# Modulation with w_mod blocks as stationary operands, first projections chunk by chunk, one SSD product per head for both directions

## The chip, the cores and the metric

The kernel runs on one core of a Trainium2 chip. TensorE is called PE here, VectorE DVE, ScalarE ACT, GpSimd POOL, and SP issues the transfers. The metric is the device time of one execution in microseconds; the time given for a kernel is the median of several runs.

## The reference

A two-layer generator backbone over 1024 latent tokens and 256 context tokens of width 1024. Per layer:

```python
mod_l = jax.nn.silu(c) @ w_mod[l] + b_mod[l]          # and mod_c from c_ctx: 3 x 1024 columns
h_l = rmsnorm(x, norm_w[l]) * (1.0 + sc_l) + sh_l     # h_c likewise for the context
(fu, fg, q, k, v, ag, z, xbc, dt, gt) = jnp.split(h @ w_in[l], split_at, axis=-1)
# Fourier mixing of fu, differential attention of q, k, v, SSD of xbc and dt,
# each times silu of its gate path; merged by sigmoid(gt), projected, added to x
```

The SSD runs in both directions over chunks of 128 positions (2 groups of 4 heads, head width 64). Its part inside a chunk is

```python
cb = jnp.einsum('bclgn,bcsgn->bcgls', cc, bc)
y_diag = jnp.einsum('bcgls,bgrcls,bcsgrp->bclgrp', cb, lmat, x * dt)   # lmat = exp of decay, triangular
y = y_f + rev(y_b) + d_skip[:, None] * xs
```

The context goes first through the SSD; in layer 1 (the last) only its final states are used, not its outputs.

## The kernel before

All activations live in 28 slots of 128 x 1288 fp32 (tiles `ar`). Projections are computed with both operands split into an f16 high and an f16 low part: each pair of 128x128 weight tile and activation block gives three f16 matmuls (`acc3`), and `projT` for a chunk of 512 tokens is 8 blocks of these, 24 matmuls. Weights arrive as fp32 in `raw`, and are squared, scaled and split into `w` by ACT and DVE (`fetch`). The 1280 tokens are ten tiles in three chunks: 512, 512 and the context's 256.

Instructions are not issued in the order of the code. Five generators (m: the main branches; p: projections; f: merges and the layer's end; e: gates; g: modulation of layer 1) hand operations to a list scheduler in Python, which keeps a model clock per engine, gives each operation a priority (its number minus `BIAS` of its thread; weights are `w`), lets a generator run until `AHEAD` operations of it are pending, and places PSUM banks. DVE and ACT may wait for a nearly ready operation of higher priority (`HOLD`). What it writes out is fixed: each engine then runs its list in order on the chip. So a changed cost or table moves instructions everywhere.

At the start (`mod0`), for each of eight blocks k of the contraction, two 128x1024 pieces of w_mod arrive: `part` 1 (scale) and 0 (shift). For part 1 and k < 7 DVE accumulates piece times the per-partition value of silu(c) for both conditions in `acc`; the rest goes to PE with the 128x2 block of silu(c) as the stationary operand and 512 columns of w_mod moving, and gives rows of 2 x 1024. `partition_sums` (products with a column of ones) and 16 transposes bring both into columns; `mod_finish` makes `ab`, the scale and bias by which ACT turns transposed, normalized x into h (`norm_T`), and DVE splits h into high (a cast) and low (a subtraction). Chunk 0 is handled in thread p (tiles `scrp`), the other two in f (`scrf`). `proj_fu` projects the Fourier inputs, one half of a weight tile at a time over all chunks.

In `ssd_scan` each chunk loads the decay rows of both directions and four heads (`rv`, 128 x 2 x 4 x 128), ACT makes relu and exp of them, DVE multiplies by the upper and lower triangle of C and B's product (`cb`), and PE multiplies each of the eight 128x128 blocks (stationary) with x times dt (`xd`, in `scrm`), forward and backward accumulating in one place of `y`.

Of the kernel before, what the change touches and what calls it, by code (L numbers as in the profile page):

```python
# [14 lines left out]
AF = mybir.ActivationFunctionType  # L15
ALU = mybir.AluOpType
# [20 lines left out]
U_SC = 2.0 ** -16  # L37
# [6 lines left out]
NSLOT = 28  # L44
NW = 8
RAW = 2
BIAS = {'m': 1200, 'p': 400, 'w': 600, 'f': 0, 'e': -50000, 'g': -100000}
AHEAD = {'m': 100, 'p': 150, 'f': 40, 'e': 54, 'g': 6}
MAXB = {'m': 4, 'p': 3, 'f': 3, 'e': 1, 'w': 1, 'g': 1}
LEAST = (1, 1)  # L50
WLIM = {'p': 2, 'f': 4, 'e': 1}
# [366 lines left out]
class Builder:  # L418
# [281 lines left out]
    def mod_finish(self, L, modT):  # L700

        V, l = self.nc.vector, L.l
        pv = self.pv[l]
        V.tensor_tensor(modT, modT, pv[:, 0:16].unsqueeze(2).to_broadcast([128, 16, 2]), ALU.add)
        ab = self.cst.tile([128, 2, 8, 2], F32, name=f"ab{l}")
        V.scalar_tensor_tensor(ab[:, 0], modT[:, 8:16, :], 1.0,
                               pv[:, 24:32].unsqueeze(2).to_broadcast([128, 8, 2]), ALU.add, ALU.mult)
        V.tensor_copy(ab[:, 1], modT[:, 0:8, :])
        f = ab.rearrange("p a k s -> p (a k s)")
        sq = self.small(32)  # L710
        V.tensor_tensor(sq, f, f, ALU.mult)
# [12 lines left out]
        V.tensor_scalar(f, f, S, None, ALU.mult)
        L.ab = ab
# [8 lines left out]
    def mod0(self, L):  # L734

        nc, V = self.nc, self.nc.vector
        row, acc = [self.alloc(), self.alloc()], [self.alloc(), self.alloc()]
        p = [[self.mm(True), self.mm(True)] for _ in range(2)]
        nc.bias['w'] = 0
        for k in range(8):  # L740
            for part in (1, 0):
                yield ('slots', 1)
                s = self.alloc()
                nc.sync.dma_start(s.v(1024), self.A['wm'][0, part, k])
                for i in range(2):
                    if part and k < K_DVE:
                        a, c = acc[i].v(1024), self.cs[:, k, i:i + 1]
                        if k == 0:
                            V.tensor_scalar(a, s.v(1024), c, None, ALU.mult)
                        else:  # L750
                            V.scalar_tensor_tensor(a, s.v(1024), c, a, ALU.mult, ALU.add)
                    else:
                        self.mul(p[part][i][:2], self.cs[:, k], s.v(1024)[:, i * 512:i * 512 + 512], k == K_DVE * part, k == 7)
                s.drop()
            if k == 1:
                self.consts()
            if k == 3:
# [6 lines left out]
            if k == K_DVE:
                t = self.mm(True)
                self.partition_sums(acc, t[:, 32:48])
        for part in range(2):
            for i in range(2):
                nc.scalar.activation(row[part].v(1024)[:2, i * 512:i * 512 + 512], p[part][i][:2], AF.Copy)
            for b in range(8):  # L770
                nc.tensor.transpose(t[:, 16 * part + 2 * b:16 * part + 2 * b + 2], row[part].v(1024)[:2, b * 128:b * 128 + 128], self.ident[:2, :2])
        modT = self.cst.tile([128, 16, 2], F32, name="modT0")
        V.tensor_copy(modT.rearrange("p b s -> p (b s)"), t[:, :32])
        V.tensor_tensor(modT[:, 8:].rearrange("p b s -> p (b s)"), modT[:, 8:].rearrange("p b s -> p (b s)"), t[:, 32:48], ALU.add)
        for r in row + acc:
            r.drop()
# [69 lines left out]
    def norm_T(self, L, tiles, xt):  # L846
# [5 lines left out]
        for d in range(8):  # L852
            p = self.tp()
            for i in range(n):
                self.tr(p[:, i * 128:i * 128 + 128], xt[i].v(1024)[:, d * 128:d * 128 + 128])
            t = self.scr() if n > 2 else self.scr2()
            nc.scalar.activation(t[:, :n * 128], p[:, :n * 128], AF.Identity,
                                 scale=L.ab[:, 0, d, st:st + 1], bias=L.ab[:, 1, d, st:st + 1])
            h = L.hT[d][:, :, t0:t0 + n * 128]
            nc.vector.tensor_copy(h[:, 0], t[:, :n * 128])  # L860
            nc.vector.tensor_tensor(h[:, 1], t[:, :n * 128], h[:, 0], ALU.subtract)
            yield
        for s in xt:
# [342 lines left out]
    def toff(t):  # L1206
        return t * 128 if t < 8 else 1028 + (t - 8) * 128

    def conv_block(self, L, w, half, d, blk, res):

        nc, V = self.nc, self.nc.vector
        cp = self.pv[L.l][:, 33 + 6 * blk:39 + 6 * blk]
        yield ('slots', 1)
        xin = self.alloc()
        xv = xin.v(1288)
        for a, b in ((0, 2), (1026, 1030), (1286, 1288)):
            nc.gpsimd.memset(xv[:, a:b], 0.0)
        for c0, cn in CH_ALL:
            p = self.projT(w, L.hT, half, c0, cn)
            o = c0 + 2 if c0 < 1024 else 1030  # L1220
            nc.scalar.activation(xv[:, o:o + cn], p[:, :cn], AF.Copy, scale=d)
            yield
        yield ('slots', 1)
        acc = self.alloc()
        av = acc.v(1284)
        nc.scalar.activation(av, xv[:, 0:1284], AF.Identity, scale=cp[:, 0:1], bias=cp[:, 5:6])
        for k in range(1, 5):
            V.scalar_tensor_tensor(av, xv[:, k:k + 1284], cp[:, k:k + 1], av, ALU.mult, ALU.add)
        nc.scalar.activation(xv[:, 0:1284], av, AF.Tanh)
        V.scalar_tensor_tensor(av, xv[:, 0:1284], 1.0, av, ALU.add, ALU.mult)  # L1230
        xin.drop()
        res.append(acc)

    def ssd_in(self, L, g):
# [25 lines left out]
        r = []  # L1260
# [5 lines left out]
        for t0 in range(0, NT, 4):  # L1266
# [3 lines left out]
                o = self.toff(t0 + i)  # L1270
                self.tr(p[:, i * 128:i * 128 + 128], G.BT.v(1284)[:, o:o + 128])
            nc.scalar.activation(G.bn[:, t0:t0 + tn].rearrange("p t n -> p (t n)"), p[:, :tn * 128], AF.Copy)
        yield from self.conv_block(L, w, 1, d, 6 + g, r)
        G.CT = r[1]
        self.done(L, f'bc{g}')
        yield ('need', (L.l, 'w', f'z{g}'))
# [11 lines left out]
    def ssd_scan(self, L, g):  # L1288
# [30 lines left out]
        for c in [8, 9, 0, 1, 2, 3, 4, 5, 6, 7]:  # L1319
            if c < L.nt:  # L1320
# [7 lines left out]
                for dr in range(2):  # L1328
                    for h in range(4):
                        nc.scalar.activation(rv[:, dr, h], rv[:, dr, h], AF.Relu, scale=-1.0, bias=av[:, dr, h:h + 1])  # L1330
                nc.scalar.activation(row.v(1024), row.v(1024), AF.Exp, scale=-1.0)
                p = self.alt()
                self.mul(p[:, :128], G.BT.v(1284)[:, o:o + 128], G.CT.v(1284)[:, o:o + 128], True, True)
                cb = self.scr()
                V.tensor_tensor(cb[:, 0:128], p[:, :128], self.U, ALU.mult)
                V.tensor_tensor(cb[:, 128:256], p[:, :128], self.L, ALU.mult)
                for dr in range(2):
                    V.tensor_tensor(rv[:, dr], rv[:, dr], cb[:, dr * 128:dr * 128 + 128].unsqueeze(1).to_broadcast([128, 4, 128]),
                                    ALU.mult)
                xd = self.scr()  # L1340
                xdv = xd.rearrange("p (d h q) -> p d h q", d=2, h=4)
                for dr in range(2):
                    V.tensor_tensor(xdv[:, dr], G.x[c].rearrange(h4, q=64), bc4(L.dt, c, dr), ALU.mult)
                yield 5.0
                y, y2 = self.alt(), self.alt()
                for h in range(4):
                    for dr in range(2):
                        self.mul(y[:, h * 64:h * 64 + 64], rv[:, dr, h], xdv[:, dr, h], dr == 0, dr == 1)
                row.drop()
                if H is not None:  # L1350
                    self.mul(y2[:, 256:512], G.CT.v(1284)[:, o:o + 128], H, True, True)
# [75 lines left out]
    def proj_fu(self, L, pair):  # L1427
# [4 lines left out]
        nc.vector.tensor_tensor(cy[:, 0:1], inv, L.inv_h, ALU.mult)  # L1432
        nc.vector.tensor_scalar(cy[:, 1:2], cy[:, 0:1], 2.0 ** 13 * 2.0 ** -7.5, None, ALU.mult)
        nc.vector.tensor_scalar(cy[:, 0:1], cy[:, 0:1], 2.0 ** 13 * 2.0 ** -8.5, None, ALU.mult)
        for j in range(2):
            yield ('slots', 1)
            u = self.alloc()
            for c0, cn in L.chunks:
                yield ('need', (L.l, f'h{c0 // 512}'))
                p = self.projT(w, L.hT, j, c0, cn)  # L1440
                nc.scalar.activation(u.v(1280)[:, c0:c0 + cn], p[:, :cn], AF.Copy, scale=U_SC)
                yield
            L.u[2 * pair + j] = (u, cy)
# [657 lines left out]
```

## Time and profile before

| | |
|---|---|
| median of 3 runs | 2614.3 us (2610.61 to 2615.71) |
| the profiled execution | 2615.48 us, span 2613.7 us |
| mean granted clock of PE | 0.980 of 2.4 GHz |
| busy: PE, DVE, ACT, POOL | 2501.8, 1828.2, 1252.1, 33.7 us |

The span is the time from the first instruction to the last in the profiled execution. Busy time counts an engine once where instructions overlap. A group's busy time is its share of that; its mean is the duration of one instruction by itself, which for pipelined matmuls is longer than what each adds. An fp32 matmul is counted as two instructions. All helpers record at line 400, so groups are told apart by tiles.

### The profile page before, as it was taken

What the parts mean: (1) busy time and instruction counts of PE and PEld (TensorE: products, weight loads), DVE (VectorE), ACT (ScalarE), POOL (GpSimd) and SP (SyncE); (2) the same over time, 40 slices, a digit from 0 to 9 for tenths busy, and PEclk for the clock granted to TensorE, in tenths of its full rate; (3) what the DMA queues carried; (4) which work ended last, traced back from release to release, by engine and by line L of the source; (5) the groups of instructions that cost most, each with busy time, mean ns of one, the idle gap of its engine ahead of it and who ended that gap; (6) DMA issues with size and microseconds to landing.
All of it is one profiled execution on the core that took longest, in us unless ns stands there. A gap on an engine that the chain in (4) does not pass through costs nothing. (4 is left out here: it accounts for less than half of the span.)

```text
span 2613.7 us, 42499 instructions
## 1 busy us (share of the span) xinstructions
PE 2501.8 (96%) x16962; PEld 1565.2 (60%) x16962; DVE 1828.2 (70%) x3783; ACT 1252.1 (48%) x2260; POOL 33.7 (1%) x78
## 2 busy tenths in 40 slices
PE   5999999999999999999999999999999899999998
PEld 2556655666665476576588546545655457556567
DVE  6785665677888468468866687776676748558766
ACT  4543545536654455445423464464544645446321
POOL 0000000000000000000000000000000000000000
PEclk8999999999999999999999999999999899999999
DMA  6331333344356223213632123434342412222451
GB/s 247 112 101 53 86 82 94 90 143 110 84 129 179 68 77 115 68 53 102 230 137 97 43 83 74 111 93 99 98 91 62 123 57 73 93 88 94 155 180 65
DMA packets 256978, 270.61 MB, mean 104 GB/s; under 512 B 181062, under 2 KB 191110, under 8 KB 256780
## 3 DMA queue, kind: packets, MB, share of 16 engines
q1 hardware_dynamic: 256780, 267.89, 34.6%
q8 instruction: 133, 2.18, 0.3%
q14 instruction: 65, 0.53, 0.1%
HBM read 178.02 MB, written 36.88 MB: 82 GB/s over the span
## 5 line engine op out<-in xcount | busy, mean ns | idle before, releaser
L400 PE MATMUL ps<-ar,w 128*128 128x512 f16 (+1 forms) x7200 | 1463.1, 356 | 9.4 <-ACT w L400 6.1
L400 PEld LDWEIGHTS <-w 128*128 128x128 f16 x7200 | 699.5, 98 | 643.0 <-issue 20.3
L400 PEld LDWEIGHTS <-ar 128*128 128x128 f16 x8144 | 668.1, 98 | 256.7 <-issue 36.7
L400 PE MATMUL ps<-ar,ar 128*128 128x128 f16 (+4 forms) x4420 | 555.9, 277 | 24.7 <-ACT ar L400 14.1
L400 PE MATMUL ps<-w,ar 128*128 128x256 f16 x3312 | 400.8, 273 | 0.4 <-ACT ar L400 0.4
L400 ACT ACTIVATE ar<-ps,s1m,qksc 128x1280 f32<-128x1280 f32 (+1 forms) x144 | 190.1, 1320 | 196.9 <-DVE s1m L400 134.1
L400 DVE TENSOR_REDUCE s1m<-ps 128x1 f32<-128x1280 f32 (+1 forms) x144 | 197.0, 1368 | 92.5 <-PE ps L400 91.8
L400 ACT ACTIVATE w<-raw 128x1024 f16<-128x1024 f32 x145 | 152.4, 1051 | 128.1 <-PE ps L400 75.3
L400 ACT ACTIVATE ar<-ar 128x1280 f16<-128x1280 f32 (+4 forms) x140 | 153.8, 1100 | 102.0 <-DVE ar L400 91.8
L400 DVE SCALAR_TENSOR_TENSOR ar<-ar,pv,ar 128x1284 f32<-128x1284 f32 x64 | 99.4, 1554 | 64.9 <-ACT ar L400 63.5
L400 DVE TENSOR_TENSOR ar<-ar,ar 128x1280 f16<-128x1280 f32 (+3 forms) x116 | 123.4, 1065 | 13.9 <-ACT ar L400 13.5
L400 PE MATMUL ps<-scrm,ar 128*128 128x64 f32 (+1 forms) x720 | 122.3, 305 | 7.1 <-issue 3.3
L400 ACT ACTIVATE ar<-ps 128x128 f32<-128x128 f32 (+6 forms) x196 | 69.7, 387 | 115.4 <-PE ps L400 114.3
L400 ACT ACTIVATE ar<-ps,ds 128x512 f32<-128x512 f32 (+1 forms) x88 | 54.7, 624 | 140.8 <-PE ps L400 136.0
L400 PEld LDWEIGHTS ps<-scrm,ar 128*128 128x128 f32 x720 | 99.1, 198 | 35.2 <-DVE scrm L400 18.4
L400 PE MATMUL ps<-k,ar 128*128 128x128 f32 (+2 forms) x540 | 88.6, 292 | 27.6 <-DVE ar L400 25.9
L400 DVE SCALAR_TENSOR_TENSOR ar<-ar,ps 128x512 f32<-128x512 f32 (+1 forms) x116 | 64.3, 562 | 65.1 <-ACT ar L400 47.8
L400 PEld LDWEIGHTS ps<-k,ar 128*128 128x128 f32 (+1 forms) x540 | 68.8, 163 | 61.6 <-DVE ar L400 31.0
L400 DVE SCALAR_TENSOR_TENSOR ar<-ar,s1m,ar 128x1280 f32<-128x1280 f32 (+1 forms) x72 | 103.1, 1432 | 0.0
L400 ACT ACTIVATE ar<-ar,ar 128x128 f32<-128x128 f32 x288 | 88.1, 388 | 24.3 <-DMA ar<-rows 21.0
L400 DVE SCALAR_TENSOR_TENSOR w<-raw,s1p,w 128x1024 f16<-128x1024 f32 x71 | 89.1, 1279 | 11.3 <-ACT w L400 11.2
L400 ACT ACTIVATE scrf<-ps,ds 128x512 f32<-128x512 f32 (+1 forms) x80 | 51.2, 639 | 86.2 <-PE ps L400 65.2
(215 smaller groups left out, 2049.3 us busy)
## 6 DMA issues: line engine op xcount, KB each, us to landing
raw<-in_wt SPq DMA_DIRECT2D x160, 512.0 KB, 4.6
ar<-in_wm SPq DMA_DIRECT2D x48, 512.0 KB, 5.4
ar<-rows SPq DMA_DIRECT2D x36, 512.0 KB, 3.8
yp<-scrf SPq DMA_DIRECT2D x64, 256.0 KB, 2.3
ar<-in_x SPq DMA_DIRECT2D x20, 512.0 KB, 9.4
gs<-scre SPq DMA_DIRECT2D x32, 256.0 KB, 2.8
scrf<-yp SPq DMA_DIRECT2D x32, 256.0 KB, 2.7
ar<-ar SPq DMA_DIRECT2D x32, 160.0 KB, 2.8
```

The source lines that it names most:

```text
L400: o.fn(*(place(a) for a in o.args), **{k: place(a) for k, a in o.kw.items()})
```

## The change

1. `mod0`: every 128x128 block of both parts is the stationary operand of a product with the 128x2 block of silu(c); all accumulate in 32 columns of one PSUM tile, which a product with a zero operand clears first. The DVE sums, the partition sums, the transposes and the row copies go; the bias is added in the copy out.
2. `norm_T`: the cast of h is done by POOL for groups of four tiles (chunks 0 and 1).
3. `proj_fu`: chunk by chunk, both halves of the weight tile in each chunk.
4. `conv_block`: for C, in layer 1, without the context chunk.
5. `ssd_scan`: forward and backward relu are summed (each is zero where the other counts), so one exp and one decay block serve both directions; `cb` is multiplied with dt of each head and direction beforehand, and each head needs one product, with x itself moving.
6. The scheduler's numbers: `BIAS`, `AHEAD`, `HOLD`, `X_AT`, `W_AT`.

```diff
-BIAS = {'m': 1200, 'p': 400, 'w': 600, 'f': 0, 'e': -50000, 'g': -100000}
-AHEAD = {'m': 100, 'p': 150, 'f': 40, 'e': 54, 'g': 6}
+BIAS = {'m': 1200, 'p': 300, 'w': 1000, 'f': 0, 'e': -50000, 'g': -100000}
+AHEAD = {'m': 120, 'p': 120, 'f': 40, 'e': 27, 'g': 6}
...
-HOLD = 0.4
-X_AT, W_AT, K_DVE = 3, 6, 7
+HOLD = 0.25
+X_AT, W_AT = 4, 7
...
     def mod0(self, L):
...
+        t = self.mm(True)
         nc.bias['w'] = 0
+        zero = self.small(32)
+        nc.gpsimd.memset(zero, 0.0)
...
-                for i in range(2):
-                    if part and k < K_DVE:
-                        a, c = acc[i].v(1024), self.cs[:, k, i:i + 1]
...
-                            V.scalar_tensor_tensor(a, s.v(1024), c, a, ALU.mult, ALU.add)
-                    else:
-                        self.mul(p[part][i][:2], self.cs[:, k], s.v(1024)[:, i * 512:i * 512 + 512], k == K_DVE * part, k == 7)
+                if k == 0 and part:
+                    self.mul(t[:, 0:32], s.v(1024)[:, 0:128], zero, True, False)
+                for b in range(8):
+                    c = 16 * part + 2 * b
+                    self.mul(t[:, c:c + 2], s.v(1024)[:, b * 128:b * 128 + 128], self.cs[:, k], False, k == 7 and not part and b == 7)
...
-            h = L.hT[d][:, :, t0:t0 + n * 128]
-            nc.vector.tensor_copy(h[:, 0], t[:, :n * 128])
+            (nc.gpsimd if n > 2 else nc.vector).tensor_copy(h[:, 0], t[:, :n * 128])
...
-        yield from self.conv_block(L, w, 1, d, 6 + g, r)
+        yield from self.conv_block(L, w, 1, d, 6 + g, r, L.chunks)
...
-                nc.scalar.activation(row.v(1024), row.v(1024), AF.Exp, scale=-1.0)
+                V.tensor_tensor(rv[:, 0], rv[:, 0], rv[:, 1], ALU.add)
+                nc.scalar.activation(row.v(1024)[:, 0:512], row.v(1024)[:, 0:512], AF.Exp, scale=-1.0)
...
-                for dr in range(2):
-                    V.tensor_tensor(rv[:, dr], rv[:, dr], cb[:, dr * 128:dr * 128 + 128].unsqueeze(1).to_broadcast([128, 4, 128]),
-                                    ALU.mult)
-                xd = self.scr()
-                xdv = xd.rearrange("p (d h q) -> p d h q", d=2, h=4)
-                for dr in range(2):
-                    V.tensor_tensor(xdv[:, dr], G.x[c].rearrange(h4, q=64), bc4(L.dt, c, dr), ALU.mult)
+                for h in range(4):
+                    dtf, dtb = (L.dt[:, c, dr * 8 + g * 4 + h:dr * 8 + g * 4 + h + 1] for dr in range(2))
+                    nc.scalar.activation(rv[:, 1, h], cb[:, 0:128], AF.Copy, scale=dtf)
+                    V.scalar_tensor_tensor(rv[:, 1, h], cb[:, 128:256], dtb, rv[:, 1, h], ALU.mult, ALU.add)
+                V.tensor_tensor(rv[:, 0], rv[:, 0], rv[:, 1], ALU.mult)
...
                 for h in range(4):
-                    for dr in range(2):
-                        self.mul(y[:, h * 64:h * 64 + 64], rv[:, dr, h], xdv[:, dr, h], dr == 0, dr == 1)
+                    self.mul(y[:, h * 64:h * 64 + 64], rv[:, 0, h], G.x[c][:, h * 64:h * 64 + 64], True, True)
...
+        u = [self.alloc(), self.alloc()]
+        for c0, cn in L.chunks:
+            yield ('need', (L.l, f'h{c0 // 512}'))
+            for j in range(2):
+                p = self.projT(w, L.hT, j, c0, cn)
+                nc.scalar.activation(u[j].v(1280)[:, c0:c0 + cn], p[:, :cn], AF.Copy, scale=U_SC)
+                yield
```

The order on PE where the first projections meet the last transposes, before. `k` is the identity, `ar_72` and `ar_73` are the context's tiles, `ar_80` the first block of h, `w_92` the first half of the first weight tile.

```order
L400 LDWEIGHTS w_92
L400 MATMUL ps<-ar_80,w_92 128x512
L400 MATMUL ps<-k_140,ar_72 128x128 x3
L400 MATMUL ps<-k_140,ar_73 128x128 x3
L400 MATMUL ps<-k_140,ar_72 128x128
L400 MATMUL ps<-k_140,ar_73 128x128
```

After; here `ar_90`, `ar_91`, `ar_74` are the first blocks of h, `w_93` is the second half of the weight tile, `ar_68` to `ar_71` are tiles of chunk 1.

```order
L400 MATMUL ps<-ar_90,w_93 128x512
L400 MATMUL ps<-k_140,ar_68 128x128
L400 MATMUL ps<-k_140,ar_69 128x128
L400 MATMUL ps<-k_140,ar_70 128x128
L400 MATMUL ps<-k_140,ar_71 128x128
L400 LDWEIGHTS w_93
L400 MATMUL ps<-ar_90,w_93 128x512
L400 LDWEIGHTS w_93
L400 MATMUL ps<-ar_91,w_93 128x512
```

Before, four projection products stand ahead of the context's transposes; after, 53 stand ahead of the last block of h of chunk 0, in both halves and two chunks, and the context's transposes come behind them.

The order on DVE from the scalings of chunk 1 on, before (`scrp` is chunk 0, `scrf` chunk 1).

```order
L400 TENSOR_SCALAR ar_71<-ar_71,s10f 128x1024
L400 TENSOR_TENSOR ar_80<-scrp,ar_80 128x512
L400 CAST ar_81<-scrp 128x512
L400 TENSOR_TENSOR ar_81<-scrp,ar_81 128x512
L400 CAST ar_80<-scrf 128x512
L400 CAST ar_81<-scrf 128x512
L400 TENSOR_TENSOR ar_80<-scrf,ar_80 128x512
L400 TENSOR_TENSOR ar_81<-scrf,ar_81 128x512
L400 CAST ar_82<-scrp 128x512
L400 CAST ar_82<-scrf 128x512
```

After, at the same place.

```order
L400 TENSOR_SCALAR ar_71<-ar_71,s10f 128x1024
L400 TENSOR_TENSOR ar_91<-scrp,ar_91 128x512
L400 TENSOR_TENSOR ar_74<-scrp,ar_74 128x512
L400 SCALAR_TENSOR_TENSOR w_93<-raw,s1p,w_93 128x1024
L400 TENSOR_TENSOR ar_90<-scrf,ar_90 128x512
L400 TENSOR_TENSOR ar_91<-scrf,ar_91 128x512
L400 TENSOR_TENSOR ar_75<-scrp,ar_75 128x512
L400 TENSOR_TENSOR ar_76<-scrp,ar_76 128x512
L400 TENSOR_TENSOR ar_74<-scrf,ar_74 128x512
```

The casts are gone from DVE's list, and the split of the weight's second half (`w_93`; that of `w_92` stands 17 rows ahead of it) is now among the subtractions; before, the split of `w_92` came behind all sixteen.

The order on PE in an SSD chunk, before (`scrm` is x times dt, `ar_72` the decay blocks, `H` the state).

```order
L400 MATMUL ps<-ar_86,ar_77 128x512
L400 MATMUL ps<-scrm,ar_72 128x64
L400 MATMUL ps<-H,ar_74 128x256
L400 MATMUL ps<-scrm,ar_72 128x64 x7
L400 LDWEIGHTS ar_77
L400 MATMUL ps<-ar_86,ar_77 128x512
```

After (`ar_88` the decay blocks, `ar_71` is x).

```order
L400 MATMUL ps<-ar_67,w_97 128x512
L400 MATMUL ps<-ar_71,ar_88 128x64 x4
L400 MATMUL ps<-H,ar_64 128x256
L400 MATMUL ps<-ar_66,ar_64 128x256
L400 LDWEIGHTS w_97
L400 MATMUL ps<-ar_67,w_97 128x512
```

Eight products of 64 columns became four, with the same stationary shape.

## Rows read from the trace of the kernel before

**Rows 1.** Page, busy time of the engines and share of the span.

```profile
PE 2501.8 (96%) x16962; PEld 1565.2 (60%) x16962; DVE 1828.2 (70%) x3783; ACT 1252.1 (48%) x2260; POOL 33.7 (1%) x78
```

**Rows 2.** Busy time in three stretches: start us : end us total, then PE, PEld, DVE, ACT, POOL.

```profile
0.00:75.00 75.00, 46.10 (x189) 23.89 (x190) 53.75 (x134) 35.44 (x58) 0.55 (x5) 0.80 0.57 222
75.00:2560.00 2485.00, 2412.22 (x16378) 1502.52 (x16376) 1737.56 (x3520) 1207.44 (x2186) 33.15 (x73) 0.99 0.35 100
2560.00:2613.70 53.70, 43.53 (x399) 38.76 (x397) 36.87 (x130) 9.20 (x16) 0.00 (x0) 0.94 0.20 79
```

**Rows 3.** What PE waited for over the span: us, times, longest us.

```profile
PE ps L400 <- DVE ar L400: 26.2, 12, 10.4
...
PE ps L400 <- DVE scrm L400: 3.2, 9, 0.9
```

**Rows 4.** PE groups by form: engine, operation, tiles, shape, count | busy us, mean ns | idle.

```profile
L400 PE MATMUL ps<-scrm,ar 128*128 128x64 f32 x576 | 77.1, 280 | 3.3 <-issue 3.3
...
L400 PE MATMUL ps<-w,ar 128*128 128x256 f16 x3312 | 400.8, 273 | 0.4 <-ACT ar L400 0.4
```

**Rows 5.** Timeline of PE in one SSD chunk: start us, us, operation, count [idle before].

```profile
978.72 0.39 PE L400 MATMUL ps<-scrm,ar 128*128 128x64 f32 x2
978.95 0.65 PE L400 MATMUL ps<-H,ar 128*128 128x256 f32 x2
979.43 1.67 PE L400 MATMUL ps<-scrm,ar 128*128 128x64 f32 x14
980.94 0.87 PE L400 MATMUL ps<-ar,ar 128*128 128x256 f32 x3
```

**Rows 6.** Timeline of PE, ACT and DVE in the first 75 us.

```profile
4.93 1.42 DVE L400 TENSOR_SCALAR ar<-ar,cs 128x1024 f32<-128x1024 f32 x2 [1.79 <-DMA ar<-in_wm]
...
34.47 6.71 PE L400 MATMUL ps<-k,ar 128*128 128x1 f32 x48
...
42.91 11.70 PE L400 MATMUL ps<-k,ar 128*128 128x128 f32 x64
...
44.21 1.46 ACT L400 ACTIVATE scrp<-ps,ab 128x512 f32<-128x512 f32 x2 [0.31 <-DVE cy L400]
...
46.55 2.74 DVE L400 TENSOR_SCALAR ar<-ar,s10f 128x1024 f32<-128x1024 f32 x4
...
51.60 1.28 DVE L400 TENSOR_TENSOR ar<-scrf,ar 128x512 f16<-128x512 f32 x2
...
65.52 0.69 DVE L400 TENSOR_TENSOR ar<-scrp,ar 128x512 f16<-128x512 f32 x1
...
67.42 3.64 PE L400 MATMUL ps<-k,ar 128*128 128x128 f32 x16 [10.40 <-DVE ar L400]
...
67.85 1.28 DVE L400 SCALAR_TENSOR_TENSOR w<-raw,s1p,w 128x1024 f16<-128x1024 f32 x1
...
70.85 4.42 PE L400 MATMUL ps<-ar,w 128*128 128x512 f16 x19
```

**Rows 7.** Two us of the 128x1 passes; the figure behind POOL's is PE's granted clock.

```profile
38.00:40.00 2.00, 2.00 (x14) 1.98 (x14) 0.00 (x0) 1.59 (x4) 0.00 (x0) 0.50 1.05 410
```

**Rows 8.** POOL group by form.

```profile
L400 POOL COPY ar<-ar 64x1280 f16<-64x1280 f16 x8 | 11.4, 1423 | 1522.3 <-DMA ar<-ar 1130.3 <-DVE ar L400 269.8 <-PE ps L400 122.2
```

**Rows 9.** DVE groups by form.

```profile
L400 DVE TENSOR_TENSOR ar<-ar,scrm 128x512 f32<-128x512 f32 x72 | 46.1, 681 | 0.0
...
L400 DVE TENSOR_TENSOR scrm<-ar,ar 128x256 f32<-128x256 f32 x144 | 59.4, 419 | 4.1 <-ACT scrm L400 2.4
...
L400 DVE TENSOR_TENSOR ar<-ar 128x512 f32<-128x512 f32 x16 | 10.3, 686 | 3.7 <-ACT ar L400 3.7
...
L400 DVE SCALAR_TENSOR_TENSOR ar<-scrm,cy,ar 128x128 f32<-128x128 f32 x16 | 6.5, 449 | 0.0
```

**Rows 10.** ACT groups by form.

```profile
L400 ACT ACTIVATE ar<-ar,ar 128x128 f32<-128x128 f32 x288 | 88.1, 388 | 24.3 <-DMA ar<-rows 21.0 <-DVE scrm L400 2.9
...
L400 ACT ACTIVATE ar<-ar 128x1024 f32<-128x1024 f32 x36 | 37.8, 1051 | 0.6
```

More of the change, by code (lines that the diff above doesn't have):

```diff
@@ L703, in mod_finish @@
         pv = self.pv[l]
-        V.tensor_tensor(modT, modT, pv[:, 0:16].unsqueeze(2).to_broadcast([128, 16, 2]), ALU.add)
+        if l:
+            V.tensor_tensor(modT, modT, pv[:, 0:16].unsqueeze(2).to_broadcast([128, 16, 2]), ALU.add)
         ab = self.cst.tile([128, 2, 8, 2], F32, name=f"ab{l}")
@@ L736, in mod0 @@
         nc, V = self.nc, self.nc.vector
-        row, acc = [self.alloc(), self.alloc()], [self.alloc(), self.alloc()]
-        p = [[self.mm(True), self.mm(True)] for _ in range(2)]
+        t = self.mm(True)
         nc.bias['w'] = 0
+        zero = self.small(32)
+        nc.gpsimd.memset(zero, 0.0)
         for k in range(8):
@@ L744, in mod0 @@
                 nc.sync.dma_start(s.v(1024), self.A['wm'][0, part, k])
-                for i in range(2):
-                    if part and k < K_DVE:
-                        a, c = acc[i].v(1024), self.cs[:, k, i:i + 1]
-                        if k == 0:
-                            V.tensor_scalar(a, s.v(1024), c, None, ALU.mult)
-                        else:
-                            V.scalar_tensor_tensor(a, s.v(1024), c, a, ALU.mult, ALU.add)
-                    else:
-                        self.mul(p[part][i][:2], self.cs[:, k], s.v(1024)[:, i * 512:i * 512 + 512], k == K_DVE * part, k == 7)
+                if k == 0 and part:
[3 more added lines that the diff above has]
+                    self.mul(t[:, c:c + 2], s.v(1024)[:, b * 128:b * 128 + 128], self.cs[:, k], False, k == 7 and not part and b == 7)
                 s.drop()
@@ L763, in mod0 @@
                 self.prefetch()
[L764 to L771, printed above, removed]
         modT = self.cst.tile([128, 16, 2], F32, name="modT0")
[L773 to L776, printed above, removed]
+        V.tensor_tensor(modT, t[:, :32].rearrange("p (b s) -> p b s", s=2), self.pv[0][:, 0:16].unsqueeze(2).to_broadcast([128, 16, 2]), ALU.add)
         nc.close('p', True)
@@ L1207, in toff, with conv_block @@
         return t * 128 if t < 8 else 1028 + (t - 8) * 128
-    def conv_block(self, L, w, half, d, blk, res):
+    def conv_block(self, L, w, half, d, blk, res, chunks=CH_ALL):
         nc, V = self.nc, self.nc.vector
@@ L1215, in conv_block @@
         xv = xin.v(1288)
-        for a, b in ((0, 2), (1026, 1030), (1286, 1288)):
+        for a, b in ((0, 2), (1026, 1030), (1286, 1288))[:len(chunks)]:
             nc.gpsimd.memset(xv[:, a:b], 0.0)
-        for c0, cn in CH_ALL:
+        for c0, cn in chunks:
             p = self.projT(w, L.hT, half, c0, cn)
@@ L1224, in conv_block @@
         acc = self.alloc()
-        av = acc.v(1284)
-        nc.scalar.activation(av, xv[:, 0:1284], AF.Identity, scale=cp[:, 0:1], bias=cp[:, 5:6])
+        n = 1284 if len(chunks) == 3 else 1024
+        av = acc.v(n)
+        nc.scalar.activation(av, xv[:, 0:n], AF.Identity, scale=cp[:, 0:1], bias=cp[:, 5:6])
         for k in range(1, 5):
-            V.scalar_tensor_tensor(av, xv[:, k:k + 1284], cp[:, k:k + 1], av, ALU.mult, ALU.add)
-        nc.scalar.activation(xv[:, 0:1284], av, AF.Tanh)
-        V.scalar_tensor_tensor(av, xv[:, 0:1284], 1.0, av, ALU.add, ALU.mult)
+            V.scalar_tensor_tensor(av, xv[:, k:k + n], cp[:, k:k + 1], av, ALU.mult, ALU.add)
+        nc.scalar.activation(xv[:, 0:n], av, AF.Tanh)
+        V.scalar_tensor_tensor(av, xv[:, 0:n], 1.0, av, ALU.add, ALU.mult)
         xin.drop()
@@ L1434, in proj_fu @@
         nc.vector.tensor_scalar(cy[:, 0:1], cy[:, 0:1], 2.0 ** 13 * 2.0 ** -8.5, None, ALU.mult)
-        for j in range(2):
[L1436 to L1443, printed above, removed]
+        yield ('slots', 2)
+        u = [self.alloc(), self.alloc()]
[5 more added lines that the diff above has]
+                yield
+        for j in range(2):
+            L.u[2 * pair + j] = (u[j], cy)
             self.ev.add((L.l, f'fu{2 * pair + j}'))
```

## The prediction

> **What bounds the kernel now.** I read the page's busy times first. PE is busy 96% of the span, DVE 70%, ACT 48% [rows 1]. A busy PE can still be a slow PE, so next came the groups by form: the 576 instructions of the 64-column fp32 product share 77.1 us, 0.134 us each, and inside a chunk 14 of them start over 1.51 us, 0.108 us each [rows 4, 5]. They run back to back, and so do the f16 groups, so PE's time is work, not waiting. The three stretches then say where PE is not at work: 28.9 us of the first 75, 72.8 us of the long middle (3%), 10.2 us at the end [rows 2]. So an instruction taken from PE in the middle is worth its own duration, one taken from DVE or ACT there is worth nothing by itself, and the first 75 us are a chain of their own that has to be read from the timeline [rows 6].
>
> **The SSD product.** For each of 36 chunks (two groups, ten chunks in layer 0 and eight in layer 1) PE made eight 128x64 fp32 products, forward and backward of four heads; now four. A product is two instructions, so 288 of 576 go. Two prices: the group's busy time halved is 38.5 us [rows 4]; from start to start, a chunk's 16 instructions hold PE for 0.23 + 1.51 = 1.74 us, half of which times 36 is 31.3 us [rows 5]. The last instruction's end is modelled, which makes the first too high, and gaps make the second too low; I take the mean, 34.9 us.
>
> What pays for it: DVE loses two 512-wide products (0.64 us each) and two 256-wide ones (0.41 us each), 2.1 us a chunk, and gets a 512-wide sum, four 128-wide operations with a scalar (bounded by the 0.41 us of such a form) and one 512-wide product, 0.64 + 1.64 + 0.64 = 2.9 us [rows 9]. ACT's exp shrinks from 1.05 us to about half, and four 128-wide copies come, 0.31 us each by the nearest form [rows 10]. Both gain about 0.8 us a chunk, 30 us over the program. I cost this at nothing: what hides it is the projection and gate work that stands between the chunks on PE. PE's largest wait in the program is 26.2 us for DVE's ar tiles; for the scratch tiles of these chunks it waited 3.2 us in nine waits [rows 3]. If that cover were gone the chain would show: from the last relu to the product it was 1.05 + 1.28 = 2.3 us, and is 0.64 + 0.6 + 1.22 + 0.41 + 0.64 = 3.5 us, to be paid at every chunk that finds PE without other work.
>
> **The convolution of C in layer 1** leaves out the context chunk: 24 products of 256 columns in each of two groups, 48 x (400.8 / 3312 = 0.121 us) = 5.8 us of PE [rows 4]. Its DVE and ACT instructions get a fifth shorter; nothing waits for that.
>
> **Layer 0's modulation.** Before, DVE summed most of the scale half, PE the shift half as products with a 2-column stationary operand, and then 32 + 16 passes of PE turned both into columns (48 instructions in 6.71 us, 0.138 us each), ending at 41.1; the first h left ACT at 44.2 [rows 6]. Now PE does all 128 blocks, 256 instructions, with 128 stationary and 2 moving columns. The nearest row is that same run of 48, which has one moving column: 256 x 0.138 = 35.3 us from the first landing at 4.93, ending at 40.3, and three small DVE operations become one: ab is there at about 43.2. That gains 1 us. Bounds: at the 0.108 us of the 64-column passes [rows 5] it would end at 32.6, 8 us earlier; at the 0.183 us of the run of 64 transposes (11.70 us, waits within it counted in, rows 6 again) at 51.8, 11 us later. The clock is a live question: in the run of 48 PE was busy all the time and its granted clock was still 0.50, the 1.2 GHz level, at 14 passes in 2 us [rows 7]; so the lower level costs such passes little, and I keep 0.138.
> [...]
>
> **From h to the first projections.** This is where the start waits. Before, DVE did cast and subtraction of all 16 (tile, chunk) pairs, with the second chunk first: the last h of chunk 0 came at 66.1; the low part of the first weight tile's first half was made after that, at 67.85 to 69.1; and in front of it PE's queue held the context transposes, for which it waited 10.4 us. Projections began at 70.85, with four done earlier [rows 6]. Now the casts are on POOL, the low parts of both halves of the first weight tile stand ahead of most subtractions on DVE, and PE has 53 projection products of two weight halves and two chunks in front of the last h, the context transposes behind them (order rows in the section on the change). DVE after 43.2: two low parts at 1.28, the rsqrt chain 2.4 (44.2 to 46.55), four scalings 2.74, 16 subtractions of 0.64: 17.9 us, so h is whole at 61.1 [rows 6]. PE meanwhile: transposes 11.7 us, to 54.9, then room for 6.2 / 0.213 = 29 products (a 512-column product takes 4.42 / 19 = 0.23 us at mixed clock, 0.213 at the 2.4 GHz level). Gain: 70.85 - 61.1 = 9.75, plus (29 - 4) x 0.213 = 5.3, minus the context transposes still to do, 3.4 (67.42 to 70.85): 11.6 us. If none of the 29 fits, 5.5; if all 53 do, 16.8. POOL's cast is not in the trace. Nearest is its copy of 1280 f16 in 1.42 us [rows 8]: 0.57 us by elements, 1.14 by bytes read, 1.42 at most taken whole. Sixteen of these are 9, 18 or 23 us beside DVE's 17.9, so at the worst of them h is whole at about 69, and with all 53 products done by then the gain is still 9. I keep 11.6.
>
> **The numbers of the planner** (look-ahead of gates 54 to 27, weights' bias, hold) move every queue but add no work. Costed at nothing, bounded by the 72.8 us of idle PE in the middle: a fifth less (-15), half as much again (+36).
>
> **Sum.** 34.9 + 5.8 + 11.6 = 52.3 us. The profiled execution took 2615.5 (span 2613.7), so 2563.2; it lies 1.2 above the median of the three, so 2562.
>
> **Rivals.**
> Better: the modulation's passes go at 0.108 us and end 8 us earlier, 2554, or the middle idles less, 2547. For it: the SSD passes of the same type run at that rate. Against: the 48 did not. 0.15.
> The middle idles half as long again because gates, the work that fills PE's holes, are queued half as deep: +36, 2598. For it: DVE is 70% busy and the holes are short. Against: 27 is still one whole gate product of 24 instructions. 0.13.
> POOL's cast is slow, twice the copy row: 16 x 2.84 = 45 us, h whole at 91.5; start term (70.85 - 91.5) + 49 x 0.213 - 3.4 = -13.6 instead of +11.6: 2587. 0.07.
> A milder form: casts and DVE's subtractions shut each other out, 16 x 0.57 = 9.1 us more on DVE's chain, h at 70.2, the gain 7.7, 2566. [...] 0.05, and close enough to the forecast to count with it.
> Slower: the longer SSD chain is not covered. Place: PE in front of a chunk's four products; price up to 3.5 us a chunk where it was covered before; with half the chunks bare 18 x 3.5 = 63, 2625. It decides from 52.3 / 3.5 = 15 bare chunks of the 36. Against: 3.2 us of such waits in all now. 0.05.
> That the change doesn't take its 288 instructions off PE is excluded: the order shows four products where there were eight.
>
> **How the numbers follow.** Forecast 0.60 (with the milder form), own range 2548 to 2580. Corners of all bounds: 2615.5 - 39 - 6 - 25 - 15 = 2530 and 2615.5 - 31 - 5 + 5 + 36 = 2620. The range 2535 to 2598 leaves out the ends beyond the idle rival and beyond most of the better one. A measurement of this kernel can tell 0.2%, 5 us, from no change. Faster by more: the forecast, better, idle and POOL cases but for their tails, 0.92; within 0.2%: half-covered chain or much idle, 0.04; slower: 0.04.
>
> **What would show it.** Right: 288 instructions of 128x64 fp32 on PE with about 39 us; PE busy down by some 40 us and idle down by 10; the first projection in front of 60 us; the modulation's last pass at 40. Wrong: POOL casts over 1.5 us; PE waits on scratch tiles or ar over 1 us a chunk; idle in the middle beyond 85 us. The prediction fails if the middle's idle moves by more than 35 us either way.

## The result, and the profile after

The changed kernel takes 2583.28 us (median of 4 runs, 2582.74 to 2585.78) against 2613.3 us beside it: ratio 0.9887, 95% interval 0.987 to 0.9904. It is 30 us faster; 52 were forecast, and 2583 lies inside the range of 2535 to 2598, just above the forecast's own 2548 to 2580. The profiled execution took 2585.78 us, span 2584.0.

The page's first part after; before it is [rows 1]:

```profile
PE 2486.6 (96%) x16800; PEld 1572.5 (61%) x16800; DVE 1821.3 (70%) x3823; ACT 1268.0 (49%) x2398; POOL 47.5 (2%) x93
```

PE's busy time fell by 15.2 us, its idle time by 14.5 (111.9 to 97.4). Both are sums of larger terms of both signs. First the SSD's products by form, after; columns: group, count, busy time, mean of one in ns, idle time just before them and what ended it:

```profile
L400 PE MATMUL ps<-ar,ar 128*128 128x64 f32 x288 | 41.2, 290 | 16.0 <-DVE ar L400 15.4 <-issue 0.4 <-ACT ar L400 0.2
```

The product's busy time was 77.1 [rows 4] and is 41.2: 35.9 us less, the forecast's 34.9. But PE now stands idle 16.0 us in front of it. Next the start, PE's timeline after (start, duration, operation, count, idle time before):

```profile
5.46 54.75 PE L400 MATMUL ps<-cs,ar 128*128 128x2 f32 x256
...
61.50 4.16 PE L400 MATMUL ps<-k,ar 128*128 128x128 f32 x24
68.40 7.33 PE L400 MATMUL ps<-k,ar 128*128 128x128 f32 x36 [2.74 <-DVE ar L400]
75.80 3.83 PE L400 MATMUL ps<-ar,w 128*128 128x512 f16 x17
...
79.91 11.60 PE L400 MATMUL ps<-ar,w 128*128 128x512 f16 x53
```

The modulation's 256 passes took 54.75 us, 0.214 each where 0.138 was forecast, and end at 60.2 instead of 40.3; the first projection is at 75.8, later than before (70.85, [rows 6]). The transfers are not what holds them: from 50 to 60 us nothing is transferred and 48 passes go through, 48 or 49 as in every 10 us before. Then DVE and POOL, whose casts and subtractions make h:

```profile
62.47 0.24 DVE L400 TENSOR_SCALAR ab<-ab,s1p 128x32 f32<-128x32 f32 x1
...
70.61 1.28 DVE L400 TENSOR_TENSOR ar<-scrp,ar 128x512 f16<-128x512 f32 x2
...
75.60 2.11 DVE L400 TENSOR_TENSOR ar<-scrp,ar 128x512 f16<-128x512 f32 x2
...
86.12 0.68 DVE L400 TENSOR_TENSOR ar<-scrp,ar 128x512 f16<-128x512 f32 x1
...
64.78 1.31 POOL L400 CAST ar<-scrp 128x512 f16<-128x512 f32 x2 [3.18 <-ACT scrp L400]
...
74.07 2.08 POOL L400 CAST ar<-scrp 128x512 f16<-128x512 f32 x2
```

Alone, a cast is 0.65 us and a subtraction 0.64; side by side each takes 1.04. From the scaled ab (62.7) to the whole of h (86.8) it is 24.1 us, 17.9 forecast, 27 in the prediction's milder form. So each slows the other, 0.65 and 0.64 to 1.04; by what, no run shows. Before, DVE made the pair by itself:

```profile
54.33 0.42 DVE L400 CAST ar<-scrf 128x512 f16<-128x512 f32 x1
54.79 0.69 DVE L400 TENSOR_TENSOR ar<-scrf,ar 128x512 f16<-128x512 f32 x1
55.40 0.42 DVE L400 CAST ar<-scrf 128x512 f16<-128x512 f32 x1
```

That is 1.07 us from one cast to the next, so where the two engines ran side by side the move gained nothing: 1.04 against 1.07. From the scaled ab to the whole of h it was 22.1 us before (44.1 to 66.2), without the two low parts of the weights (1.28 each) that now stand in between.

The middle's idle time hardly moved in sum. Stretches before, then after (PE, PEld, DVE, ACT, POOL busy, granted clock, DMA):

```profile
0.00:100.00 100.00, 71.10 (x365) 39.12 (x366) 68.83 (x170) 49.72 (x81) 0.55 (x5) 0.85 0.49 186
100.00:5000.00 4900.00, 2430.74 (x16600) 1526.06 (x16597) 1759.36 (x3614) 1202.36 (x2179) 33.15 (x73) 0.99 0.18 51
```

```profile
0.00:100.00 100.00, 90.79 (x455) 78.45 (x456) 39.93 (x111) 37.75 (x61) 15.15 (x22) 0.97 0.44 172
100.00:2584.00 2484.00, 2395.84 (x16349) 1494.03 (x16346) 1781.35 (x3713) 1230.21 (x2337) 32.36 (x71) 0.98 0.34 102
```

Behind 100 us PE was idle 2613.7 - 100 - 2430.7 = 83.0 us, and is 88.2. The places changed. The last chunks of layer 1's SSD have nothing beside them now; one of them, after:

```profile
2406.32 1.19 PE L400 MATMUL ps<-scrm,ar 128*128 128x256 f32 x2 [3.57 <-ACT scrm L400]
2407.30 0.63 PE L400 MATMUL ps<-ar,ar 128*128 128x128 f32 x2
2410.96 1.97 PE L400 MATMUL ps<-ar,ar 128*128 128x64 f32 x8 [3.02 <-DVE ar L400]
2412.72 1.17 PE L400 MATMUL ps<-H,ar 128*128 128x256 f32 x2
2413.68 1.06 PE L400 MATMUL ps<-ar,ar 128*128 128x256 f32 x2
2417.70 1.19 PE L400 MATMUL ps<-scrm,ar 128*128 128x256 f32 x2 [2.96 <-ACT scrm L400]
```

In four of the last five chunks PE waits twice, 2.7 to 4.4 us each, together 25 of the 33.2 us that it is idle in front of these two groups (128x64 and `scrm` 128x256). Its granted clock is 0.50 from 2410 to 2440 besides, and the four products' eight instructions take 1.97 us there; at 1.00, in e10's chunk below, they take 1.00 us. The second wait is for the state update's x (`xw` of `step`, in `scrm`), which DVE makes behind the chunk's output (the row names an ACT instruction that ends at the same time); the change left that part of the chain as it was. In exchange holes elsewhere were filled.

### The profile page after: what moved, and what is told of

Its sections match the earlier page's. It is cut to its first block, busy times and chain, and to the rows that moved or that the text cites. A ratio compares the mean times of both kernels' runs of the same rounds, so it can differ in the third digit from the quotient of the medians.

```text
span 2584.0 us, 42400 instructions
## 1 busy us (share of the span) xinstructions
PE 2486.6 (96%) x16800; PEld 1572.5 (61%) x16800; DVE 1821.3 (70%) x3823; ACT 1268.0 (49%) x2398; POOL 47.5 (2%) x93
## 5 line engine op out<-in xcount | busy, mean ns | idle before, releaser
L400 PEld LDWEIGHTS <-ar 128*128 128x128 f16 x8000 | 648.9, 98 | 231.3 <-issue 26.4
L400 ACT ACTIVATE ar<-ar 128x1280 f16<-128x1280 f32 (+5 forms) x140 | 138.1, 987 | 104.6 <-DVE ar L400 103.0
L400 DVE SCALAR_TENSOR_TENSOR ar<-ar,pv,ar 128x1284 f32<-128x1284 f32 (+1 forms) x64 | 97.1, 1517 | 32.9 <-ACT ar L400 32.3
L400 ACT ACTIVATE ar<-ps 128x128 f32<-128x128 f32 (+5 forms) x192 | 67.3, 386 | 104.6 <-PE ps L400 103.6
L400 ACT ACTIVATE w<-raw,s1p 128x1024 f16<-128x1024 f32 x72 | 79.0, 1138 | 33.9 <-DVE s1p L400 33.7
L400 PE MATMUL ps<-k,ar 128*128 128x128 f32 (+1 forms) x492 | 79.3, 289 | 15.5 <-DVE ar L400 14.7
L400 DVE SCALAR_TENSOR_TENSOR w<-raw,s1f,w 128x1024 f16<-128x1024 f32 x65 | 81.4, 1279 | 9.8 <-ACT w L400 9.8
L400 PEld LDWEIGHTS ps<-k,ar 128*128 128x128 f32 x492 | 63.1, 157 | 38.2 <-DVE ar L400 23.3
L400 DVE SCALAR_TENSOR_TENSOR scrf<-ps,ds,ar 128x256 f32<-128x256 f32 x72 | 34.7, 482 | 72.6 <-PE ps L400 72.3
L400 PEld LDWEIGHTS ps<-ar,ar 128*128 128x128 f32 x428 | 67.0, 206 | 29.7 <-DVE ar L400 20.8
```

Of the source, the lines that this page charges most:

```text
L400: o.fn(*(place(a) for a in o.args), **{k: place(a) for k, a in o.kw.items()})
```

## The experiments

Ten kernels beside before and after. For all of them: time, the 95% interval of the ratio to before, and where PE was idle in the profiled execution (span minus busy, up to 100 us and behind it).

| kernel | median us | ratio, 95% | PE busy | idle to 100 | idle behind |
|---|---|---|---|---|---|
| before | 2613.3 | 1 | 2501.8 | 28.9 | 83.0 |
| after | 2583.3 | 0.987 to 0.9904 | 2486.6 | 9.2 | 88.2 |
| e1 heat | 2691.0 | 1.0278 to 1.0309 | 2529.0 | 13.3 | 146.4 |
| e2 old modulation | 2659.7 | 1.0158 to 1.0189 | 2486.7 | 19.6 | 152.7 |
| e3 old numbers | 2657.8 | 1.0148 to 1.0182 | 2510.1 | 10.2 | 136.2 |
| e4 SSD alone | 2600.2 | 0.9934 to 0.9963 | 2469.1 | 29.8 | 103.5 |
| e5 heat 4 (one run) | 2708.2 | none | 2538.2 | 10.9 | 157.4 |
| e6 AHEAD 28 | 2663.9 | 1.0179 to 1.0213 | 2505.6 | 9.6 | 140.8 |
| e7 before, after's numbers | 2668.7 | 1.0193 to 1.0223 | 2510.3 | 27.0 | 128.4 |
| e8 old modulation, own numbers | 2549.7 | 0.9744 to 0.9771 | 2451.8 | 20.3 | 76.1 |
| e9 before, searched numbers | 2580.1 | 0.986 to 0.9887 | 2485.5 | 29.1 | 63.8 |
| e10 after, searched numbers | 2546.0 | 0.9737 to 0.9763 | 2472.2 | 10.8 | 58.5 |

**e1_heat: more columns beside the modulation's passes.**

```diff
+        t2, heat = self.mm(True), self.wbuf[7][:, 0, 0:128].bitcast(BF16)
+        nc.gpsimd.memset(heat, 0.0)
...
+                    if b % 2:
+                        self.mul(t2, heat, s.v(1024).bitcast(BF16)[:, 1:1024:2], True, True)
```

> The kernel after, with one more product behind every second block of w_mod: 128x512 bf16, zeros as the stationary operand, into a PSUM bank that nobody reads (64 products, 13.6 us at the 0.213 us of the 2.4 GHz level). Theory 1, the 256 passes of 2 columns took 0.214 us each because PE stood at its lower level: the added columns bring the clock up, the passes take 0.107 us (27.4 us in all), and although there is more work the modulation ends EARLIER, at about 42 to 47 us instead of 60.2; first projection at about 62, whole kernel 2569 to 2575. Theory 2, 0.214 us is what such a pass costs at any clock: the passes keep their price, the modulation ends at 60.2 + 13.6 = 74, whole kernel about 2597. Theory 3, the passes wait for the transfers: the last block lands before 40 us, and the end does not move in either direction by more than 5 us.

The modulation ended at 78.3, and the kernel lost 108 us against after. By that alone theory 2 would stand. But an added product took 0.39 us to the start of the next instruction, not 0.213; before's trace has 0.43 at granted 0.50 and 0.216 at 1.00 (last section). By that pace PE had stayed at its lower level, so the trial didn't reach the question. And 58 of the 105 us by which its span is longer are idle time behind 100 us, which neither theory has.

**e5_heat4: four times as many.**

```diff
-                    if b % 2:
+                    for _ in range(2):
                         self.mul(t2, heat, s.v(1024).bitcast(BF16)[:, 1:1024:2], True, True)
```

> The kernel after with two products of 128x512 bf16 (zeros as the stationary operand) behind every block of w_mod, 256 in all. It is run for one row, what a block costs once PE streams all the time. Theory 1 (0.214 us a pass is the price at the 1.2 GHz level, the added 64 of the first trial did not lift PE from it): in a stretch at the 2.4 GHz level a period is 2 x 0.107 + 2 x 0.213 = 0.64 us; at the lower level it would be 1.28. Theory 2 (0.214 at any clock): 2 x 0.214 + 2 x 0.213 = 0.85 us at the 2.4 GHz level. The whole kernel is longer by the added work and by whatever the new plan does.

One run, 2708.2 us. PE's timeline at the start and at 60 us:

```profile
6.03 1.01 PE L400 MATMUL ps<-ar,w 128*128 128x512 bf16 x2
6.84 0.42 PE L400 MATMUL ps<-cs,ar 128*128 128x2 f32 x2
7.12 1.01 PE L400 MATMUL ps<-ar,w 128*128 128x512 bf16 x2
...
59.93 0.28 PE L400 MATMUL ps<-cs,ar 128*128 128x2 f32 x2
60.06 0.61 PE L400 MATMUL ps<-ar,w 128*128 128x512 bf16 x2
60.52 0.28 PE L400 MATMUL ps<-cs,ar 128*128 128x2 f32 x2
60.65 0.61 PE L400 MATMUL ps<-ar,w 128*128 128x512 bf16 x2
```

A block's period is 1.09 us at the start and 0.59 from about 12 us on: under the 0.64 of theory 1 and far under the 0.85 of theory 2. The two passes of a block took 0.28 us to the start of what follows at first and 0.13 later, so they about halve, while the two longer products beside them go from 0.81 to 0.46; I read that as the change of level. These passes stand between longer products, and at the lower level they cost 0.14 each there, not the 0.214 of after; that 256 in a row would cost 0.107 at the upper level is an estimate, half of 0.214, which no run shows. The added work costs more than it gives: the modulation ends at 85.4.

**e2_oldmod: the modulation of before in the kernel after.** `mod0` and `mod_finish` as in the kernel before, `X_AT, W_AT, K_DVE = 3, 6, 7`.

> The kernel after with the modulation of the kernel before (DVE sums, 2-column stationary operands, transposes; X_AT, W_AT = 3, 6). Theory 1 and 2 agree that the new modulation costs about 19 us at the start: its last pass is back at about 41, the first projection at about 60 to 64, the whole kernel at 2562 to 2567, which was the forecast. Rival, the shortfall of 21 us against the forecast is made in the middle (the last chunks of layer 1's SSD stand without other work): the start comes back but the kernel stays at 2575 or above, because what starts earlier waits longer later.

Its start came back as all expected:

```profile
36.08 5.30 PE L400 MATMUL ps<-k,ar 128*128 128x1 f32 x48
...
57.05 1.67 PE L400 MATMUL ps<-ar,w 128*128 128x512 f16 x7 [0.36 <-ACT scrf L400]
...
60.84 5.20 PE L400 MATMUL ps<-ar,w 128*128 128x512 f16 x23 [0.39 <-DVE ar L400]
```

And yet it is 76 us slower than after. PE's busy time is the same, 2486.7, though the modulation has 29 us less of it: the rest of the work took longer, at a lower clock (mean 0.964, after 0.983). Idle time behind 100 us is 152.7 instead of 88.2. The rival named the right region with far too small a size. From 700 to 800 us alone PE is idle for 40.6 us, in layer 0's attention (44.2 us of waits for ACT's `ar` tiles from 450 to 950).

**e3_oldtables and e4_ssdonly: the numbers of before on the new code, and the new product alone on the old.** e3 takes the lines `BIAS`, `AHEAD`, `HOLD` of before; e4 is before with only part 5 of the change.

> The kernel after with the planner's numbers of the kernel before (BIAS, AHEAD, HOLD). Theory A, the gates queued half as deep leave the last five chunks of layer 1's SSD bare (PE idle 48 of 80 us before 2450): with 54 ahead that stretch is filled and the kernel is 15 to 30 us faster, about 2560. Theory B, the new numbers fill holes elsewhere and the end would be bare in any case, because PE has 36 us less to do while the SSD's chain on DVE and ACT got longer: with the old numbers idle PE grows, 2590 to 2605. Forecast's term (zero): within 5 us of 2583.

> The kernel before with only the SSD product changed (one product per head). The forecast's term stands: PE loses 35 to 36 us and the longer chain hides: 2613.3 - 35 = 2578, idle PE in the middle unchanged within 6 us. Rival, the chain of a chunk (0.8 us longer on DVE and on ACT) is bare in part: 0.8 to 3.5 us a chunk comes back as idle time for DVE's ar tiles, 10 of 36 chunks bare gives +8 to +35: 2586 to 2613.

e3: theory B in direction, larger than thought: 74 us slower than after with not one instruction changed. e4: 14 us faster than before, not 35. PE's busy time is 32.7 us less, and 21.3 us come back as idle time (111.9 to 133.2). The groups of e4 name them:

```profile
L400 PE MATMUL ps<-scrm,ar 128*128 128x256 f32 x144 | 44.8, 402 | 12.5 <-ACT scrm L400 9.0 <-DVE scrm L400 2.4 <-ACT scrf L400 0.4
L400 PE MATMUL ps<-ar,ar 128*128 128x64 f32 x288 | 40.2, 286 | 16.9 <-ACT ar L400 6.8 <-DVE ar L400 6.5 <-ACT w L400 3.1
```

In front of these two groups PE was idle 3.8 + 3.3 us before and is 29.4 now: +22.3, about a third of the 63 that the prediction's slower rival gave. Only 13.6 of it is at the rival's place, the four products; 8.7 is in front of the state update, whose chain the change leaves as it was. And e4's order is made anew too, so how much is the longer chain and how much the order is not told apart here.

**e6_ahead28 and e7_newtables: is it the numbers, or any change of them?**

```diff
-AHEAD = {'m': 120, 'p': 120, 'f': 40, 'e': 27, 'g': 6}
+AHEAD = {'m': 120, 'p': 120, 'f': 40, 'e': 28, 'g': 6}
```

> The kernel after with one number of the planner changed, AHEAD of the gates 28 in place of 27: no instruction more or less. Theory P, what the three trials on the kernel after had in common (75 to 107 us lost, whatever was changed) is that the whole order is made anew and the numbers were chosen for one order: this one loses 40 to 90 us too, all of it as idle PE (and lower clock behind it) at places that have nothing to do with gates being one deeper. Theory G, the numbers act by what they say, gates queued half as deep: one more is nothing, 2578 to 2590.

> The kernel before with the planner's numbers of the kernel after (BIAS, AHEAD, HOLD). With it the four corners of code and numbers are known. Theory G, the new numbers are better ones: they gave 74 us on the new code (2657.8 to 2583.3), and give 30 to 75 here, 2540 to 2585. Theory P, they fit one code: on the old code they lose, 2640 to 2720.

Theory P in both. One more gate operation that may be pending costs 80 us, 27 to 28; and the new numbers, worth 74 us on the new code, lose 55 on the old. The stretch from 760 to 820 us says how. Groups on PE, after, then e6:

```profile
L400 PE MATMUL ps<-ar,w 128*128 128x512 f16 x141 | 32.8, 379 | 0.0
L400 PE MATMUL ps<-ar,w 128*128 128x256 f16 x72 | 9.0, 272 | 0.0
```

```profile
L400 PE MATMUL ps<-ar,ar 128*128 128x128 f16 x150 | 14.9, 288 | 3.0 <-DMA ar<-ar 2.1 <-DVE ar L400 0.9
L400 PE MATMUL ps<-ar,ar 128*128 128x512 f16 x36 | 14.0, 487 | 17.7 <-ACT ar L400 17.7
```

After has 213 projection products (`ar,w`) there, 41.8 us of work for PE while ACT makes the attention's exp. In e6 the order has put none there: PE waits 17.7 us for ACT, and its granted clock is 0.88 from 700 to 800 and 0.87 from 800 to 900 (after's is 1.00 in both).

**e8, e10 and e9: numbers made for each code.** Three codes (after with the old modulation, after, before), each with `BIAS`, `AHEAD`, `HOLD`, `X_AT`, `W_AT` of its own, in e8 also `F_FIN`. For e10:

```diff
-BIAS = {'m': 1200, 'p': 300, 'w': 1000, 'f': 0, 'e': -50000, 'g': -100000}
-AHEAD = {'m': 120, 'p': 120, 'f': 40, 'e': 27, 'g': 6}
+BIAS = {'m': 1100, 'p': 300, 'w': 400, 'f': 0, 'e': -50000, 'g': -100000}
+AHEAD = {'m': 130, 'p': 150, 'f': 50, 'e': 27, 'g': 6}
...
-HOLD = 0.25
-X_AT, W_AT = 4, 7
+HOLD = 0.33
+X_AT, W_AT = 3, 4
```

> The code of e2_oldmod (the kernel after with the modulation of before) with numbers of its own (BIAS 1100/200/400 for m/p/w, AHEAD 80/180/30/81 for m/p/f/e, HOLD 0.45, X_AT, W_AT = 4, 4, F_FIN 200), chosen among some hundreds by the end that the planner's own clock gives. Theory P, the 76 us that e2_oldmod lost were the plan's and not the modulation's: with an order made for this code PE's idle time in the middle is 60 to 90 us, the start stays some 16 us shorter than after's, and the kernel is at 2540 to 2565. Rival, the old modulation itself does harm later (its four more slots, DVE's sums): not under 2590 with any numbers.

> The kernel after, code untouched, with other numbers found in the same way (BIAS 1100/300/400, AHEAD 130/150/50/27, HOLD 0.33, X_AT, W_AT = 3, 4). Theory P: the last chunks of layer 1's SSD are no longer bare, idle PE falls by 25 to 40 us against after's 97, 2545 to 2560. Rival S, the SSD's chain got longer and is bare at the end in any order: 2578 or more.

> The kernel before, code untouched, with numbers found in the same way (BIAS 1100/250/600, AHEAD 80/135/30/81, HOLD 0.15, X_AT, W_AT = 4, 4). It says how much of a difference between two kernels here can come from numbers alone. Theory P: 2570 to 2590, 25 to 45 us faster than before, as much as the whole change brought. Rival, the numbers of before were as good as any for that code: 2605 or more.

Theory P in all three. e10, at 2546.0, is 37 us faster than after by numbers alone, and e9, the old code, reaches after's time. The same groups as of e4, in e10, and one chunk of layer 1's end:

```profile
L400 PE MATMUL ps<-scrm,ar 128*128 128x256 f32 x144 | 44.7, 401 | 3.2 <-DVE scrm L400 1.0 <-ACT scrm L400 0.6 <-ACT scre L400 0.2
L400 PE MATMUL ps<-ar,ar 128*128 128x64 f32 x288 | 37.6, 273 | 2.1 <-ACT ar L400 0.9 <-issue 0.8 <-DVE ar L400 0.2
```

```profile
2388.78 0.67 PE L400 MATMUL ps<-scrm,ar 128*128 128x256 f32 x2 [0.16 <-ACT scre L400]
2389.28 0.39 PE L400 MATMUL ps<-ar,ar 128*128 128x128 f32 x2
2389.51 3.40 PE L400 MATMUL ps<-ar,w 128*128 128x512 f16 x15
2392.74 1.00 PE L400 MATMUL ps<-ar,ar 128*128 128x64 f32 x8
2393.58 0.65 PE L400 MATMUL ps<-H,ar 128*128 128x256 f32 x2
```

The 15 projections stand where after waits 3 us for DVE; the idle time in front of the two groups is 5.3 us, as before the change (7.1). So the longer chain can be hidden, if the order leaves work for it. e8 does not get the modulation's 20 us back in the end: its start is better (at 100 us some 11 us more work is done: PE's busy time behind 100 us is 2372.1 against 2383.0), its order has 17.6 us more idle time, and the two kernels end within 4 us of each other.

## Why the prediction was right in direction and too large in size

The ledger of the profiled executions, 2615.5 to 2585.8, in us (the modulation's busy time before is its 36 row products and 48 passes, 26.0):

| term | forecast | measured |
|---|---|---|
| SSD product, PE busy | -34.9 | -35.9 |
| start: modulation's PE time 26.0 to 55.4, idle to 100 us 28.9 to 9.2 | -11.6 | +9.7 |
| convolution of C and all other busy time | -5.8 | -8.7 |
| idle in front of the SSD's two groups, 7.1 to 33.2 | 0 | +26.1 |
| idle behind 100 us elsewhere | 0 | -20.9 |
| sum | -52.3 | -29.7 |

**The SSD product** was right, price and number (288 with 41.2 us, "about 39" forecast). **The convolution's** 48 products are gone (5832 of 256 columns in f16 before, 5784 after), but that group's busy time fell by 1.9 us only, 744.9 to 743.0: each of them shares 0.1277 us before and 0.1285 after, and the row of the table holds such differences too.

**Layer 0's modulation is the step that failed.** The start term is 21.3 of the 22.6 us that are missing, since the other misses cancel, and 19.5 of the 25.7 us by which h is late are the modulation's. The step said "the lower level costs such passes little, and I keep 0.138". The passes cost 0.214, at 48 or 49 in every 10 us, and in e5 a pair of such passes fell from 0.28 to 0.13 us as PE sped up; from that I infer that PE stayed at its lower level from the first of the 256 to the last, though its row shows it busy all the time. The range of this term ended at 0.183, too low. The trace of before showed that the level matters, and I read the wrong stretch of it. Its stretches:

```profile
35.00:37.00 2.00, 2.00 (x20) 2.00 (x19) 0.16 (x1) 2.00 (x4) 0.00 (x0) 1.00 1.00 406
37.00:39.00 2.00, 2.00 (x11) 2.00 (x11) 0.00 (x0) 2.00 (x5) 0.00 (x0) 0.51 1.04 414
```

20 passes in 2 us at the upper level, 11 at the lower (0.18 each). [Rows 7] began a microsecond later, where the run's last third is another product (16 transposes of two rows), and its 14 passes looked like the mean of the run. 0.138 was a mean over two levels and two products. At 0.18 the modulation would have ended at about 52: that is 11 of the 20 us, and why two moving columns cost 0.214 where one cost 0.18 stays open.

**From h to the projections**: the milder form, a supposition that no row of before showed, came true, 6.2 us on DVE's chain where it gave 9.1. Nine of the sixteen subtractions ran at 1.04 us, which is 3.6 of it; the rest is waits and longer scalings. The POOL rival, 2.84 us a cast, fell: 1.07 at most. Projections did start in front of the whole h, as the order said. The 0.213 us at which this step counts a 512-column product is in no trace: at granted 1.00 before's has 0.216, which changes the step's 11.6 by under 0.3.

**The SSD chain, costed at nothing where it is longer,** stood bare in part of the chunks: 26 us in after and 22 in e4. In after 12.7 of this is in front of the four products (3.3 to 16.0), the slower rival's place, and 13.4 in front of the state update (3.8 to 17.2), which no rival named and whose chain did not get longer. What I named as its cover is real, but where it stands is the order's doing: after has none left for four of layer 1's last five chunks, and in e10 the idle time in front of both groups is 5.3 us with the same chain.

**The planner, costed at nothing between -15 and +36,** was the largest unknown of all and its range too narrow. On after's code idle time behind 100 us was 88.2 with after's numbers, 136.2 with before's, 140.8 with one number off by one, 58.5 at best. The measured sum stays near the forecast because after's numbers fit this code: the -20.9 in the ledger covers most of the bare chunks, two terms that the prediction did not have, and that they cancel is luck. With `BIAS`, `AHEAD` and `HOLD` of before the same code would have been slower than before by 44 us (e3 against before), outside the range and with the other sign, and no argument of the prediction excluded that. The sign was right partly for a reason that it did not have.

**The signs** that were to show it right: 288 instructions with 41.2 us and idle time 14.5 us lower came; PE's busy time fell by 15 us and not 40, the first projection is at 75.8 and not in front of 60, the modulation's last pass ends at 60.2 and not 40.

**What the code is worth** is read best with each in an order of its own: before 2580.1 (e9), after 2546.0 (e10), 34 us. In PE's time of their profiles that is 13.3 us less work (the modulation's longer passes are in it) and 23.6 us less idle time, 18.3 of it in the first 100 us. Searches found these numbers, so each is a bound: a better order may exist for either.

It stays open why the idle time jumps with such small steps; shown is mainly where. Between 700 and 1300 us, layer 0's attention and SSD, PE is idle for 49 to 75 us in each of the six kernels that lost (e1, e2, e3, e5, e6, e7) and for 13 to 38 in the others; after's and e2's largest idle time behind that is in layer 1's SSD. What is missing there (projections) was read in after and e6 only. A trial that keeps after's order and exchanges only the modulation was not made.

## What to carry to other kernels

Where a program makes the order anew from every change, a part cannot be judged by one build: give both codes an order of their own, and try neighbours of the numbers to learn the spread (here 80 us from 27 to 28) before a 1% difference is put down to an edit. Work that hides a chain is limited: name the instructions that stand in that place and count whether they last to the end. A row's mean over a run that crosses a change of clock, or two kinds of product, is no price: split the run at the change and use each side.

## What the runs showed of the hardware

PE's levels in before: at granted 1.00 five products of 512 columns went by in 1.08 us (from 104.72), 0.216 each, about 2.4 columns a ns; at 0.50 two in 0.86 (from 884.16), 0.43 each, about 1.2. These paces are what the prediction calls the 2.4 and the 1.2 GHz level; the traces give the clock only as a share.

In after PE was busy all the time for 55 us and still stayed at its lower level (256 passes of 128 stationary and 2 moving columns; that it was the lower level is inferred from e1 and e5). In e1 it stayed there for 73 us; 64 products of 512 columns stood among the passes, with 0.25 us of idle time in about 10. In e5, with 256 of them, it rose at about 12 us. The record of the granted clock says 1.00 through all of that; the pace of known products (1.01 us or 0.61 for the same pair in e5) is what shows the level there.

A cast of 512 columns on POOL took 0.65 us alone, and beside DVE's subtraction both took 1.04, so that a pair moved from one engine to two took 1.04 a tile here, not the 0.65 of the longer one. DVE alone had made the pair in 1.07.
